# First block's modulation sums on VectorE, spread over its attention, and seven 2 MB buffers for expert weights

## The chip, the cores and the metric

The kernel runs on one core of one Trainium2 chip. The metric is the device time of one execution, in microseconds (us). Times of several executions are given by their median.

## The reference

Two transformer blocks over 256 tokens of width 1024. The first mixes with stick-breaking attention (SB, 8 heads) and the HGRN2 recurrence (HG, 4 heads), merges both through sigmoid gates, and then sends each token to 4 of 32 experts. The second block's norms are scaled and shifted by a modulation vector, `c_act @ w_ada + b_ada`, that depends on `c` alone:

```python
def hybrid_mixer(x, w_in, ...):
    sq, sk, sv, hq, hf, hi, hg, gate_sb, gate_hg = split(x @ w_in)
    o_sb = stick_breaking_attention(heads(sq), heads(sk), heads(sv))
    o_hg = hgrn2_recurrence(silu(hq), 1 - f, log(f), hi)      # f from hf
    o_hg = rms_norm(o_hg) * hgrn_norm_g * sigmoid(hg)
    merged = sigmoid(gate_sb) * (o_sb @ w_branch_sb) + sigmoid(gate_hg) * (o_hg @ w_branch_hgrn)
    return merged @ w_out

def first_block(x, ...):
    h = layer_norm(ALPHA * x + hybrid_mixer(x, ...))
    return layer_norm(ALPHA * h + moe(h, 32 experts, top 4))

def second_block(x, c, ...):
    mod = silu(c) @ w_ada + b_ada
    sh1, sc1, g1, sh2, sc2, g2 = split(mod, 6)
    h = rms_norm(x, norm1_g) * (1 + sc1) + sh1
    x = x + g1 * (mixed(h) @ w_out)
    h2 = rms_norm(x, norm2_g) * (1 + sc2) + sh2
    return x + g2 * ((silu(gt) * up) @ w_down)                # gt, up from h2 @ w_gu
```

All is float32. A product of TensorE is made of three (`mm3`): each operand is split into a high and a low part of a narrower type.

## The kernel before, in words

**Phase A** is the first block's mixer. `x @ w_in` is cut into units of 256 columns, 1 MB each. For one unit SP issues the load (`unit`, L207 to L218), ACT rounds the high half (`sh`, L164), DVE subtracts the low half (`sl`, L170, two pieces of 128x1024 for one unit), and PE runs 48 matmuls (`pj`, L174 to L176). `Weights.ahead` loads and splits units ahead of their use, over a ring of `NW` = 4 buffers of 1 MB, to which 4 buffers of the pool `w2` come later. Between the projections stand the pieces of the four HGRN heads (`hg_e`, `hg_s`, `hg_o`, `hg_n`: exponentials, scores, outputs, norm) and of the stick-breaking heads (`st_z`, `st_l`, `st_v`). Then come the gates GS (`gate_s`, 4 units), the branch `w_branch_sb` (2), the gates GH with `w_branch_hgrn`, and `w_out` (4), at whose end the router's logits are made and L704 makes the last small matmuls.

**Modulation.** The first part of the second block's modulation (columns 0 to 2048 of `w_ada`) is computed inside phase A: eight blocks of 128 rows, 1 MB each. `Modulation.step_sum` (L1264) loads block `k`, scales it by the block's 128 values of `c_act` (one for each partition) on ACT and adds it into `moda` on GpSimd; `finish_sum` later adds up over the partitions with PE. `mod_step` is called after `gate_s(1)`, `gate_s(2)`, `gate_s(3)`, after each SB branch and after each GH gate; what is left is done by `mod_step(8)` ahead of `experts`.

**Phase B** runs the 32 experts. Each has six units of 2 MB (four of `w_up`, two of `w_down`), 192 units and 403 MB in all. `big_unit` (L220) gives unit `t` one of `NW2` + `NW3` = 4 + 2 buffers, from the pools `w2` and `w3`. The pool `w3` is opened with phase B, where phase A's memory is free. The first four units can be loaded in phase A, into `w2`. Then SP has the rows `lng` and `lnb` of the layer norm (L261), `bdn`, small tables, and further units; SP and PE then read the register for the overflow branch (`flag`, L1106). Phase C is the second block.

**What sets the order.** In phases A and C a scheduler orders the instructions of each engine from their data. In phase B the order of PE and SP is that of the code (`manual_schedule`).

Of the kernel before, what the change touches and what calls it, by code (L numbers as in the profile page):

```python
# [10 lines left out]
F32 = mybir.dt.float32  # L11
# [3 lines left out]
OP = mybir.AluOpType  # L15
# [4 lines left out]
D = 1024  # L20
NW = 4
NW2 = 4
NW3 = 2
ALPHA = 2.0 ** 0.25
BIG = 1.0e30
NL = 7
# [114 lines left out]
def lines(ctx, tc, **kw):  # L141
    return Lines(ctx.enter_context(tc.tile_pool(**kw)))
# [75 lines left out]


def big_unit(E, src):  # L220

    t, n = E.wturn, NW2 + NW3
    E.wturn += 1
    at = NW2 - max(0, NW2 - (6 * NE - 1 - t) // n)
    pool, name = (E.w3, "u3") if at <= t % n < at + NW3 else (E.w2, "u2")
    u = pool.tile(list(src.shape), F32, name=name)
    E.nc.sync.dma_start(u, src)
    return u
# [62 lines left out]
def phase_a(E, A, open_h1, experts):  # L291
    nc, tc = E.nc, E.tc
    with ExitStack() as ctx:
# [145 lines left out]
        def copy_n(dst, i, ps):  # L439
            nc.scalar.activation(dst[:, :, i * 256:(i + 1) * 256], ps, AF.Copy)  # L440
# [100 lines left out]

        M = Modulation(E, A, ((0, 2048),), lambda n: tm.tile([P, 512], F32, name=n, tag="sg"))

        gate_f(0, pf0)
        gate_f(1, proj_n(HF + 256))
        silu_q(0, proj_t(HQ))
# [23 lines left out]
        hg_o(2)  # L570
        hg_s(3)
        nc.scalar.activation(sqT[:, 2:4], proj_t(SQ + 256), AF.Copy, scale=0.125)
        hg_n(2)
        hg_o(3)
        st_z(0)
        copy_n(sv, 0, proj_n(SV))
        hg_n(3)
        st_z(1)
        st_l(0)
        copy_n(sv, 1, proj_n(SV + 256))  # L580
        st_v(0)
        st_l(1)
        st_z(2)
# [6 lines left out]
            split_into(nc, ogh[:, c], ogl[:, c], ohT[:, c])  # L590

        gate_g(0, proj_t(HG))
        st_v(1)
        st_z(3)
        st_l(2)
        gate_g(1, proj_t(HG + 256))
        st_v(2)
        st_l(3)

# [8 lines left out]
        wsplit.load(wsplit.at + 4)  # L608
        ectx.close()
        h1 = open_h1()  # L610
        al2 = lines(ctx, tc, name="al2", bufs=1)

        def mod_step(n=1):
            for _ in range(n):
                M.step_sum(al2)

        gate_s(1)
        mod_step()
# [14 lines left out]
        for i in range(2):  # L633
            for jj, ps in enumerate(branch(sbw, osh, osl, i)):
                d = gs[:, i * 4 + 2 * jj:i * 4 + 2 * jj + 2]
                nc.vector.tensor_tensor(d, ps, d, op=OP.mult)  # L636
            mod_step()
        meh = al.tile([P, 8, T], F32R, name="meh", tag="xTh")
        mel = al.tile([P, 8, T], F32R, name="mel", tag="xTl")
        for i in range(2):  # L640
            ee = []
            for jj in range(2):
                e = tm.tile([P, 2, T], F32, name="sg")
                sigm(e, proj_t(GH + (2 * i + jj) * 256))
                ee.append(e)
                mod_step()
            if i == 0:
                x = al.tile([P, 2, D], F32, name="xr", tag="os")
                nc.sync.dma_start(x, xsrc)
                ln = LayerNorm(E, E.c)  # L650
            for jj, ps in enumerate(branch(hgw, ogh, ogl, i)):
                c = slice(i * 4 + 2 * jj, i * 4 + 2 * jj + 2)
                nc.vector.tensor_tensor(ee[jj], ps, ee[jj], op=OP.mult)
                nc.vector.tensor_add(gs[:, c], gs[:, c], ee[jj])
                split_into(nc, meh[:, c], mel[:, c], gs[:, c])
        mod_step(8)
        X = experts(tm)
        pl = pp.tile([P, T], F32, name="big")
        X.fold_ln(pp, "one")
# [184 lines left out]
def phase_b(E, A, X, acc):  # L844
    nc, tc = E.nc, E.tc
    up_u, dn_u, bup, it = X.up_u, X.dn_u, X.bup, X.it
    with ExitStack() as ctx:
# [13 lines left out]
        rp = lines(octx, tc, name="brt", bufs=1)  # L861
        lng = row_bcast(E, rp, A["ln1_g"], D, "lng")
        lnb = row_bcast(E, rp, A["ln1_b"], D, "lnb")
        bdn = b1.tile([NE, D], F32, name="bdn")
        nc.sync.dma_start(bdn, A["expert_b_down"][0])
        loaded = load_late(E, A, b1)
        gexp, selected, counted, rest = route(E, X, rp, pp, R)
# [212 lines left out]
def swiglu(nc, tm, ps, shape, out=None):  # L1080
    g = tm.tile(shape, F32, name="swg", bufs=1)
    s = tm.tile(shape, F32, name="sws", bufs=1)
    l = tm.tile(shape, F32, name="swl", bufs=1)
    act = (out or tm).tile(shape, F32, name="act")
    sl = (slice(None),) * (len(shape) - 1)
    nc.vector.tensor_scalar(g, ps[sl + (slice(0, None, 2),)], 7.0, None, op0=OP.min)  # L1086
    sg = nc.scalar.activation(s, g, AF.Sigmoid, scale=1.702)  # L1087
    nc.vector.tensor_scalar(l, ps[sl + (slice(1, None, 2),)], 7.0, -7.0, op0=OP.min, op1=OP.max)
    nc.vector.scalar_tensor_tensor(l, l, 1.0, g, op0=OP.add, op1=OP.mult)
    sw_last[:] = [sg, nc.vector.tensor_mul(act, l, s)]  # L1090
    return act


def overflow(E, A, X, b1, pp, R, acc, hT):
# [9 lines left out]
    with ExitStack() as ctx:  # L1104
        tm = lines(ctx, tc, name="otm", bufs=1)
        with tc.If(nc.values_load(R.flag[0:1, 0:1], min_val=0, max_val=1) > 0):  # L1106
            idr = tm.tile([P, P], F32R, name="idr")
            nc.scalar.activation(idr, E.ident, AF.Copy)
            for k in range(8):
                ps = pp.tile([P, 2, T], F32, name="g")  # L1110
                for a in range(2):
                    for n, part in enumerate((R.hh, R.hl)):
                        nc.tensor.matmul(ps[:, 0, a * P:(a + 1) * P], part[:, a, k * P:(k + 1) * P], idr,
                                         start=(a + n == 0), stop=(a + n == 2))
                nc.scalar.activation(hT[:, k], ps[:, 0], AF.Identity, bias=colv(E, "l1bp", k), scale=colv(E, "l1gp", k))
            with tc.For_i(0, NE, 1) as e:
                nc.vector.tensor_scalar(at, at, 1.0, None, op0=OP.add)
                for a in range(2):
                    w8 = tm.tile([P, NE], F32, name="w8", tag="idr")
                    nc.vector.tensor_scalar(w8, it, at, None, op0=OP.is_equal)  # L1120
                    nc.vector.tensor_mul(w8, w8, over[:, a])
                    wt = tm.tile([P, 1], F32, name="wt")
                    nc.vector.tensor_reduce(wt, w8, op=OP.add, axis=mybir.AxisListType.X)
                    aT = tm.tile([P, 8, P], F32, name="oaT")
                    for b in range(2):
                        for j in range(2):
                            br = tm.tile([1, 512], F32, name="br")
                            nc.sync.dma_start(br, bup[bass.ds(e, 1), (2 * b + j) * 512:(2 * b + j + 1) * 512])
                            nc.tensor.matmul(ups[:, j], ones[0:1], br, start=True, stop=False)
                        for k in range(8):  # L1130
                            u = tm.tile([P, D], F32, name="ou")
                            nc.sync.dma_start(u, wup[bass.ds(e, 1), k // 2 * 2 * P:(k // 2 + 1) * 2 * P, b * D:(b + 1) * D]
                                              .rearrange("o (p s) c -> s (o p) c", s=2)[k % 2])
                            for j in range(2):
                                nc.tensor.matmul(ups[:, j], hT[:, k, a * P:(a + 1) * P], u[:, j * 512:(j + 1) * 512],
                                                 start=False, stop=(k == 7))
                        act = swiglu(nc, b1, ups, [P, 2, 256], tm)
                        ps = pp.tile([P, 4, P], F32, name="t")
                        for j in range(4):
                            nc.tensor.transpose(ps[:, j], act[:, j // 2, (j % 2) * P:(j % 2 + 1) * P], E.ident)  # L1140
                        nc.scalar.activation(aT[:, 4 * b:4 * b + 4], ps, AF.Copy)
                    ys = [pp.tile([P, 512], F32, name="y", bufs=2) for _ in range(2)]
                    for c in range(8):
                        u = tm.tile([P, D], F32, name="ou")
                        nc.sync.dma_start(u, wdn[bass.ds(e, 1), c * P:(c + 1) * P, :].rearrange("o p c -> (o p) c"))
                        for j in range(2):
                            nc.tensor.matmul(ys[j], aT[:, c], u[:, j * 512:(j + 1) * 512], start=(c == 0), stop=(c == 7))
                    for j in range(2):
                        d = acc[:, a, j * 512:(j + 1) * 512]
                        nc.vector.scalar_tensor_tensor(d, ys[j], wt, d, op0=OP.mult, op1=OP.add)  # L1150
# [100 lines left out]
class Modulation:  # L1251
# [12 lines left out]
    def step_sum(self, pool):  # L1264

        nc, E = self.E.nc, self.E
        if not self.todo:
            return
        for k, u in self.load():
            if k == 0:  # L1270
                self.acc = pool.tile([P, self.n], F32, name="moda")
                nc.scalar.activation(self.acc, u, AF.Copy, scale=E.cact[:, 0:1])
            else:
                nc.scalar.activation(u, u, AF.Copy, scale=E.cact[:, k:k + 1])
                nc.gpsimd.tensor_tensor(self.acc, self.acc, u, op=OP.add)

    def finish_sum(self, pp, tag):
        nc, E, n = self.E.nc, self.E, self.n // 4
# [577 lines left out]
```

## Time and profile before

| | |
|---|---|
| three runs | 1573.3, 1574.02, 1581.15 us; median 1574.02 |
| profiled execution | 1583.92 us |
| its span | 1582.1 us |
| PE busy | 1472.4 us (93%), 8282 matmuls |
| DVE busy | 607.1 us (38%) |
| ACT busy | 418.4 us (26%) |
| GpSimd (POOL) busy | 72.9 us (5%) |
| read from memory | 516.46 MB |
| mean granted clock of PE | 0.962 |

The span is what the trace covers; the execution's own time is 1.8 us longer. Busy shares are means over phases that differ: phase A ends near 260 us and the experts' weights have landed by 1195 us. [...] L12 is line 12 of the kernel; `out<-in` are its names.

### The profile page before, as it was taken

The page shows a single profiled execution, that of the slowest core. Times are in us where ns is not written, and L with a number is a line of the kernel's source. Part 1 is how long each engine was busy: PE and PEld are TensorE (multiplying, and loading weights), DVE is VectorE, ACT ScalarE, POOL GpSimd, SP SyncE. Part 2 cuts the span into 40 slices and gives each one's busy share as a digit, 9 for nine tenths or more (in the row PEclk, how much of TensorE's full clock was granted, in tenths as well). Part 3 has the DMA queues.
Part 4 walks back from the last instruction along what each step waited for, and adds up shares of the span by engine and source line. Part 5 has one row for each costly group of instructions (what it writes and reads, how often), then busy time and mean ns, then how long its engine had stood idle before and what let it go on. Part 6 is the DMA issues. An engine that isn't in the chain of part 4 may idle for free.

```text
span 1582.1 us, 19654 instructions
## 1 busy us (share of the span) xinstructions
PE 1472.4 (93%) x8282; PEld 853.9 (54%) x8282; DVE 607.1 (38%) x1037; ACT 418.4 (26%) x675; POOL 72.9 (5%) x101
## 2 busy tenths in 40 slices
PE   8999699999989989999999999899897999999998
PEld 7999697333333333333333333233233876799998
DVE  6886877122111111211211211211215676665544
ACT  6558454001000000000001000000002565554442
POOL 0001512100000000000000000000000000000000
PEclk9999788999999999999999999999999998999999
DMA  8336766999999999999999999999998753275551
GB/s 294 125 102 236 265 207 260 374 422 430 430 429 429 430 429 430 430 429 429 430 430 429 430 429 430 430 430 429 430 430 304 248 194 107 94 253 187 187 187 54
DMA packets 106829, 518.84 MB, mean 328 GB/s; under 512 B 8144, under 2 KB 70352, under 8 KB 80112
## 3 DMA queue, kind: packets, MB, share of 16 engines
q1 hardware_dynamic: 106736, 517.53, 81.3%
q8 instruction: 67, 1.10, 0.3%
q14 instruction: 26, 0.21, 0.0%
HBM read 516.46 MB, written 1.05 MB: 327 GB/s over the span
## 4 chain that ended last, share of the span: by engine, by line
PE 59%; DMA 18%; DVE 2%; ACT 1%; issue 0%; DVEq 0%; ACTq 0%
PE up L989 20%; DMA u<-in_expert_w_down_dram 18%; PE y L1017 11%; PE y L1029 4%; PE gu L174 3%; PE gu L175 3%; PE gu L176 3%; PE g L951 2%; PE pd L174 1%; PE pd L175 1%; PE pd L176 1%; PE pj L174 1%; PE up L983 1%; PE pj L176 1%; PE pj L175 1%; PE o L1661 1%
## 5 line engine op out<-in xcount | busy, mean ns | idle before, releaser
L989 PE MATMUL up<-u,xg 128*64 128x512 f32 x2048 | 470.3, 601 | 1.7 <-DMA u<-in_expert_w_up_dram 1.7
L1017 PE MATMUL y<-u,aT 128*64 128x512 f32 x1024 | 267.1, 652 | 53.0 <-DMA u<-in_expert_w_down_dram 51.7
L989 PEld LDWEIGHTS up<-u,xg 128*64 128x64 f32 x2048 | 135.6, 137 | 265.5 <-issue 253.5
L170 DVE TENSOR_TENSOR sl<-u,sh 128x1024 fp32r<-128x1024 f32 (+3 forms) x160 | 208.4, 1308 | 120.2 <-ACT sh L164 118.9
L1017 PEld LDWEIGHTS y<-u,aT 128*64 128x64 f32 x1024 | 87.5, 149 | 231.2 <-issue 184.6
L164 ACT ACTIVATE sh<-u 128x1024 fp32r<-128x1024 f32 (+3 forms) x160 | 164.8, 1036 | 167.1 <-PE pj L175 39.6
L1086 DVE TENSOR_SCALAR swg<-up 128x512 f32<-128x512 f32 x32 | 22.1, 692 | 311.0 <-PE up L989 311.0
L1023 DVE COPY ys<-y 128x512 f32<-128x512 f32 x16 | 11.1, 692 | 276.6 <-PE y L1017 276.6
L174 PE MATMUL gu<-hTh,sh 128*128 128x256 f32 x352 | 99.5, 283 | 2.1 <-ACT modr L1307 2.1
L175 PE MATMUL gu<-hTl,sh 128*128 128x256 f32 x352 | 99.6, 283 | 0.0
L176 PE MATMUL gu<-hTh,sl 128*128 128x256 f32 x352 | 99.5, 283 | 0.0
L1087 ACT ACTIVATE sws<-swg 128x512 f32<-128x512 f32 x32 | 20.1, 629 | 262.9 <-DVE swg L1086 262.8
L1022 ACT ACTIVATE ys<-y 128x512 f32<-128x512 f32 x16 | 9.6, 597 | 280.7 <-PE y L1017 280.7
L1031 DVE TENSOR_TENSOR acc<-acc,y 128x512 f32<-128x512 f32 x62 | 42.7, 688 | 92.9 <-PE y L1029 92.9
L174 PE MATMUL pj<-xTh,sh 128*128 128x256 f32 x256 | 72.9, 285 | 4.6 <-DVE gs L636 4.6
L176 PE MATMUL pj<-xTh,sl 128*128 128x256 f32 x256 | 71.9, 281 | 0.0
L175 PE MATMUL pj<-xTl,sh 128*128 128x256 f32 x256 | 71.9, 281 | 0.0
L174 PEld LDWEIGHTS gu<-hTh,sh 128*128 128x128 f32 x352 | 68.2, 194 | 2.6 <-ACT modr L1307 2.6
L175 PEld LDWEIGHTS gu<-hTl,sh 128*128 128x128 f32 x352 | 66.8, 190 | 0.0
L176 PEld LDWEIGHTS gu<-hTh,sl 128*128 128x128 f32 x352 | 66.8, 190 | 0.0
L1029 PE MATMUL y<-ys,G 128*128 128x512 f32 x124 | 61.5, 618 | 0.0
L1007 ACT ACTIVATE aT<-t 128x512 f32<-128x512 f32 x32 | 19.1, 597 | 135.9 <-PE t L1005 135.9
(463 smaller groups left out, 2214.8 us busy)
## 6 DMA issues: line engine op xcount, KB each, us to landing
u<-in_expert_w_up_dram SPq DMA_DIRECT2D x128, 2048.0 KB, 18.8
u<-in_expert_w_down_dram SPq DMA_DIRECT2D x64, 2048.0 KB, 18.7
u<-in_w_in_dram SPq DMA_DIRECT2D x30, 1024.0 KB, 5.9
u<-in_w_ada_dram SPq DMA_DIRECT2D x24, 1024.0 KB, 6.3
u<-in_w_gu_dram SPq DMA_DIRECT2D x22, 1024.0 KB, 5.0
u<-in_w_down_dram SPq DMA_DIRECT2D x11, 1024.0 KB, 4.9
u<-in_w_out_dram SPq DMA_DIRECT2D x8, 1024.0 KB, 6.2
u<-in_w_branch_sb_dram SPq DMA_DIRECT2D x2, 1024.0 KB, 8.5
```

The costliest lines, as they stand in the source:

```text
L164: nc.scalar.activation(hi, src, AF.Copy)
L170: e.tensor_tensor(lo, src, hi, op=OP.subtract)
L174: nc.tensor.matmul(out, a[0], b[0], start=start, stop=False)
L175: nc.tensor.matmul(out, a[0], b[1], start=False, stop=False)
L176: nc.tensor.matmul(out, a[1], b[0], start=False, stop=stop)
L951: nc.tensor.matmul(ps[:, j], part[:, a, cs_], dm[:, a].rearrange("p e s -> p (e s)"), start=(n == 0), stop=(n == 7))
L989: nc.tensor.matmul(ps[i * 64:(i + 1) * 64, b].rearrange("q (m r) -> q m r", r=4), xgs[e // 4][:, k, sl], w.rearrange("p (m i r) -> p i m r ...
L1017: nc.tensor.matmul(y[oh][i * 64:(i + 1) * 64], aTs[e + i][:, 2 * b + r % 2, (r // 2) * 64:(r // 2 + 1) * 64], dn_u[e + i, b][:, r, oh * 51 ...
L1029: nc.tensor.matmul(pc, Gs[e // 2][:, a * P:(a + 1) * P], ys[:, oh], start=True, stop=True)
L1031: nc.vector.tensor_tensor(acc[:, a, c], acc[:, a, c], pc, op=OP.add)
L1086: nc.vector.tensor_scalar(g, ps[sl + (slice(0, None, 2),)], 7.0, None, op0=OP.min)
L1087: sg = nc.scalar.activation(s, g, AF.Sigmoid, scale=1.702)
```

## The change

`step_sum` does one instruction on VectorE for each block: the first scales block 0 into `moda`, the others multiply a block by its column of `c_act` and add `moda`. Five of the eight steps stand in the attention, three behind the gates GS. `NW3` becomes 3 and the units go round seven buffers in turn. To make room, `moda` lies in the pool `al`, `bdn` on a buffer of `ys`, swiglu's `swl` in `act`, and `br` (of the overflow branch) on `ou`.

```diff
-NW3 = 2
+NW3 = 3
 def big_unit(E, src):
-    t, n = E.wturn, NW2 + NW3
+    pool, name = (E.w2, "u2") if E.wturn % (NW2 + NW3) < NW2 else (E.w3, "u3")
     E.wturn += 1
-    at = NW2 - max(0, NW2 - (6 * NE - 1 - t) // n)
-    pool, name = (E.w3, "u3") if at <= t % n < at + NW3 else (E.w2, "u2")
...
         M = Modulation(E, A, ((0, 2048),), lambda n: tm.tile([P, 512], F32, name=n, tag="sg"))
+        def mod_step(n=1):
+            for _ in range(n):
+                M.step_sum(al)
...
         nc.scalar.activation(sqT[:, 2:4], proj_t(SQ + 256), AF.Copy, scale=0.125)
+        mod_step()
...
         copy_n(sv, 0, proj_n(SV))
+        mod_step()
...
         copy_n(sv, 1, proj_n(SV + 256))
+        mod_step()
...
         gate_g(0, proj_t(HG))
+        mod_step()
...
         gate_g(1, proj_t(HG + 256))
+        mod_step()
...
-        al2 = lines(ctx, tc, name="al2", bufs=1)
-        def mod_step(n=1):
-            for _ in range(n):
-                M.step_sum(al2)
         gate_s(1)
         mod_step()
...
                 nc.vector.tensor_tensor(d, ps, d, op=OP.mult)
-            mod_step()
...
                 ee.append(e)
-                mod_step()
...
-        mod_step(8)
         X = experts(tm)
...
-        bdn = b1.tile([NE, D], F32, name="bdn")
+        bdn = tm.tile([NE, D], F32, name="bdn", tag="ys", bufs=1)
...
-    l = tm.tile(shape, F32, name="swl", bufs=1)
-    act = (out or tm).tile(shape, F32, name="act")
+    l = act = (out or tm).tile(shape, F32, name="act")
...
-                            br = tm.tile([1, 512], F32, name="br")
+                            br = tm.tile([1, 512], F32, name="br", tag="ou")
...
             if k == 0:
                 self.acc = pool.tile([P, self.n], F32, name="moda")
-                nc.scalar.activation(self.acc, u, AF.Copy, scale=E.cact[:, 0:1])
+                nc.vector.tensor_scalar(self.acc, u, E.cact[:, 0:1], None, op0=OP.mult)
             else:
-                nc.scalar.activation(u, u, AF.Copy, scale=E.cact[:, k:k + 1])
-                nc.gpsimd.tensor_tensor(self.acc, self.acc, u, op=OP.add)
+                nc.vector.scalar_tensor_tensor(self.acc, u, E.cact[:, k:k + 1], self.acc, op0=OP.mult, op1=OP.add)
```

What this moves, as each engine's instructions stand in a row. SP at the attention before; `w_in` are the units of phase A, `w_ada` the modulation's blocks:

```order
L216 DMA u<-in_w_in_dram 128x8x256 x2
L216 DMA u<-in_consts_dram 128x1152
L216 DMA u<-in_w_in_dram 128x8x256 x14
L216 DMA u<-in_w_branch_sb_dram 128x4x512
L216 DMA u<-in_w_ada_dram 128x2048
L216 DMA u_1676<-in_w_ada_dram 128x2048
```

All fourteen `w_in` units stand ahead of the first `w_ada` block. The same place of SP now:

```order
L216 DMA u<-in_w_in_dram 128x8x256 x2
L216 DMA u<-in_consts_dram 128x1152
L216 DMA u<-in_w_in_dram 128x8x256 x7
L216 DMA u<-in_w_ada_dram 128x2048
L216 DMA u<-in_w_in_dram 128x8x256
L216 DMA u<-in_w_ada_dram 128x2048
L216 DMA u<-in_w_in_dram 128x8x256
L216 DMA u<-in_w_ada_dram 128x2048
L216 DMA u<-in_w_in_dram 128x8x256
L216 DMA u<-in_w_ada_dram 128x2048
L216 DMA u<-in_w_in_dram 128x8x256
L216 DMA u<-in_w_ada_dram 128x2048
```

The first five `w_ada` blocks now stand between `w_in` units; the other three follow ahead of the second unit of `w_branch_sb`, and none is left among the branches and the gates GH.

SP at the end of phase A before; `u` are units of 2 MB, `lng` waits for PE's L704:

```order
L227 DMA u_2621<-in_expert_w_up_dram 128x4096
L227 DMA u_2623<-in_expert_w_up_dram 128x4096
L1157 DMA kgrp<-in_consts_dram 128x128
L227 DMA u_2794<-in_expert_w_up_dram 128x4096
L261 DMA lng<-in_ln_g_dram 128x1024
L261 DMA lnb<-in_ln_b_dram 128x1024
L865 DMA bdn<-in_expert_b_down_dram 32x1024
L1160 DMA inv<-in_consts_dram 128x16
L1162 DMA ropeg<-in_ropeg_dram 128x64
L1164 DMA posi<-in_positions_dram 128x2x1
L227 DMA u_2796<-in_expert_w_up_dram 128x4096
L227 DMA u_2929<-in_expert_w_up_dram 128x4096
```

Five units stand ahead of `lng` (the first two of them above the rows shown), three behind it. The same place of SP now:

```order
L224 DMA u_2613<-in_expert_w_up_dram 128x4096
L733 DMA sraw<-in_consts_dram 128x64
L863 DMA bdn<-in_expert_b_down_dram 32x1024
L1157 DMA inv<-in_consts_dram 128x16
L1159 DMA ropeg<-in_ropeg_dram 128x64
L1161 DMA posi<-in_positions_dram 128x2x1
L258 DMA lng<-in_ln_g_dram 128x1024
L258 DMA lnb<-in_ln_b_dram 128x1024
L224 DMA u_2783<-in_expert_w_up_dram 128x4096
L224 DMA u_2785<-in_expert_w_up_dram 128x4096
L224 DMA u_2787<-in_expert_w_up_dram 128x4096
L224 DMA u_2919<-in_expert_w_up_dram 128x4096
```

Now four units stand ahead of `lng` (the first row is the fourth) and four behind it, and `bdn` with the small tables has moved ahead of it.

DVE inside the HGRN heads before (`ex`, `mk`, `sc` are a head's scores, `sl` the split of a weight, `sq`, `rs` a norm):

```order
L460 TENSOR_TENSOR ex<-ex,qT 128x128
L475 TENSOR_TENSOR mk<-mk 128x512
L476 TENSOR_TENSOR mk<-mk 128x256
L477 TENSOR_TENSOR sc<-mk 128x128
L474 TENSOR_TENSOR mk<-big,ksmask 128x1024
L170 TENSOR_TENSOR sl<-u,sh 128x1024
L475 TENSOR_TENSOR mk<-mk 128x512
L476 TENSOR_TENSOR mk<-mk 128x256
L147 TENSOR_SCALAR sq<-one 128x256
L477 TENSOR_TENSOR sc<-mk 128x128
```

Only the head's work and the weights' splits stand there. The same place of DVE now:

```order
L457 TENSOR_TENSOR ex<-ex,qT 128x128
L472 TENSOR_TENSOR mk<-mk 128x512
L1271 SCALAR_TENSOR_TENSOR moda<-u,cact,moda 128x2048
L473 TENSOR_TENSOR mk<-mk 128x256
L170 TENSOR_TENSOR sl<-u,sh 128x1024
L474 TENSOR_TENSOR sc<-mk 128x128
L147 TENSOR_SCALAR sq<-one 128x256
L471 TENSOR_TENSOR mk<-big,ksmask 128x1024
L150 TENSOR_TENSOR sq<-sq,rs 128x256
L472 TENSOR_TENSOR mk<-mk 128x512
```

The second step of `moda` stands inside a head's chain, ahead of a split and of `sc`.

## Rows read from the trace of the kernel before

**Rows 1.** Windows by stage: window, length, busy us of engines, granted clock, DMA share, GB/s.

```profile
57.00:100.00 43.00, 42.80 (x340) 40.85 (x339) 41.19 (x90) 19.57 (x34) 0.00 (x0) 1.00 0.27 88
100.00:158.00 58.00, 58.00 (x468) 53.25 (x467) 38.05 (x56) 44.63 (x57) 6.10 (x6) 1.00 0.56 197
158.00:260.00 102.00, 85.64 (x660) 81.94 (x659) 72.25 (x75) 47.93 (x61) 29.36 (x11) 0.87 0.67 247
260.00:289.00 29.00, 26.77 (x118) 13.57 (x120) 20.50 (x50) 9.27 (x13) 11.76 (x22) 0.82 0.70 261
289.00:1195.00 906.00, 845.82 (x3548) 296.50 (x3546) 159.21 (x261) 72.55 (x119) 18.59 (x51) 0.96 1.01 428
1195.00:1582.00 387.00, 364.07 (x2780) 320.52 (x2776) 236.90 (x434) 188.10 (x335) 3.34 (x5) 0.98 0.53 177
```

**Rows 2.** Waits of PE, 289 to 1195 us: total us, times, longest us.

```profile
PE y L1017 <- DMA u<-in_expert_w_down_dram: 51.7, 23, 3.9
```

**Rows 3.** Chain that ended last, in order of time: start us, us, what.

```profile
1174.56 19.92 DMA u<-in_expert_w_down_dram
```

**Rows 4.** Timeline of SP, 198 to 263 us: start us, us, queue, line, operation, count.

```profile
202.88 1.48 SPq L227 DMA_DIRECT2D u<-in_expert_w_up_dram  x1
...
245.65 0.39 SPq L227 DMA_DIRECT2D u<-in_expert_w_up_dram  x1
...
259.92 0.33 SPq L261 DMA_DIRECT2D lng<-in_ln_g_dram  x1
```

**Rows 5.** Line L1106 on SP's queue: ns min/median/max, first and last start us, forms.

```profile
L1106 SPq EVENT_SEMAPHORE  x10: 17/17/28, 279.0 to 288.6; - x10
```

**Rows 6.** Waits of PE, 150 to 262 us.

```profile
PE pj L176 <- DVE sl L170: 8.8, 1, 8.8
PE pj L174 <- DVE gs L636: 4.6, 1, 4.6
PE pj L174 <- ACT sg L366: 1.9, 1, 1.9
```

**Rows 7.** Line L1275 on POOL, columns of rows 5.

```profile
L1275 POOL TENSOR_TENSOR moda<-moda,u x7: 4568/4664/5298, 152.3 to 207.1; 128x2048 f32<-128x2048 f32 x7
```

**Rows 8.** Timeline of POOL: start us, us, engine, line, operation, count, idle before.

```profile
157.14 9.95 POOL L1275 TENSOR_TENSOR moda<-moda,u 128x2048 f32<-128x2048 f32 x2 [0.18 <-ACT u L1274]
...
178.17 4.92 POOL L1275 TENSOR_TENSOR moda<-moda,u 128x2048 f32<-128x2048 f32 x1 [0.57 <-ACT u L1274]
```

**Rows 9.** Timeline of DVE, same columns.

```profile
162.64 6.66 DVE L170 TENSOR_TENSOR sl<-u,sh 128x1024 fp32r<-128x1024 f32 x2
...
175.53 8.65 DVE L170 TENSOR_TENSOR sl<-u,sh 128x1024 fp32r<-128x1024 f32 x2
```

**Rows 10.** DVE groups by form, 57 to 150 us: busy us, mean ns, idle before.

```profile
L170 DVE TENSOR_TENSOR sl<-u,sh 128x1024 fp32r<-128x1024 f32 x20 | 24.4, 1222 | 7.5 <-ACT sh L164 7.4
...
L514 DVE SCALAR_TENSOR_TENSOR ss<-big,su 128x768 f32<-128x768 f32 x4 | 3.8, 956 | 3.4 <-ACT su L513 3.3
...
L170 DVE TENSOR_TENSOR ogl<-ohT,ogh 128x512 fp32r<-128x512 f32 x2 | 1.4, 688 | 0.7 <-ACT ogh L164 0.7
...
L367 DVE TENSOR_SCALAR gs<-gs 128x512 f32<-128x512 f32 x2 | 0.9, 427 | 2.5 <-ACT gs L366 2.5
```

**Rows 11.** Windows of 10 us in the gates' stage, columns of rows 1.

```profile
160.00:170.00 10.00, 1.77 (x8) 1.78 (x9) 10.00 (x5) 3.85 (x6) 7.01 (x2) 0.60 0.05 11
170.00:180.00 10.00, 10.00 (x81) 10.00 (x81) 6.55 (x5) 7.18 (x7) 6.43 (x2) 0.89 1.04 407
180.00:190.00 10.00, 5.39 (x30) 5.23 (x30) 7.64 (x5) 1.72 (x3) 3.09 (x1) 0.66 0.90 311
200.00:210.00 10.00, 10.00 (x91) 10.00 (x90) 9.47 (x10) 8.47 (x10) 2.86 (x1) 1.00 1.11 379
220.00:230.00 10.00, 10.00 (x64) 10.00 (x63) 6.89 (x12) 4.42 (x6) 0.00 (x0) 0.67 0.19 54
230.00:240.00 10.00, 10.00 (x73) 10.00 (x73) 4.85 (x7) 3.99 (x5) 0.00 (x0) 0.82 0.56 210
```

**Rows 12.** DVE groups by form, 150 to 220 us.

```profile
L170 DVE TENSOR_TENSOR sl<-u,sh 128x1024 fp32r<-128x1024 f32 x19 | 40.5, 2149 | 9.6 <-ACT sh L164 9.6
```

**Rows 13.** DMA issues on the page: line, engine, operation, count, KB each, us to landing.

```profile
u<-in_w_ada_dram SPq DMA_DIRECT2D x24, 1024.0 KB, 6.3
```

## Prediction

> **What bounds the kernel now.** I read the windows by stage first [rows 1]; the reader should see there two different limits. From 289 to 1195 us the DMA share is 1.01 at 428 GB/s: the expert weights stream and nothing else sets that stretch. PE waits in it for down weights 23 times, 51.7 us in all [rows 2], and the chain of waits ends it with the last down unit, issued at 1174.56 and 19.92 us on its way, so the stream ends at 1194.48 [rows 3]. The tail of 387 us behind it is the second block. Ahead of it lie 289 us whose limit is PE: 57 to 158 it is busy without a gap at a granted clock of 1.00. The stage of 158 to 260 differs: PE busy 85.64 of 102 us, clock 0.87, GpSimd 29.36. Phase A ends at 259.92, when SP, held until PE's last small matmuls are done, issues `lng` [rows 4]. What comes earlier there moves the whole stream and the tail with it, since the stream is a fixed 905.7 us (288.6 to 1194.48) [rows 3, 5] for 184 units of 2 MB.
>
> **Why 158 to 260 is slow.** PE's waits there [rows 6] are 8.8 us for DVE's `sl` split, 4.6 for DVE's `gs` product and 1.9 for ACT's `sg`: 15.3 us. The split is late because seven GpSimd adds of `moda` stand in that stage, each 4.6 to 5.3 us long [rows 7]. Put the timelines of the two engines side by side [rows 8, 9]: two adds run from 157.14 to 167.09, and in the same time two `sl` splits take 6.66 us; an add starts at 178.17, and two splits begun at 175.53 take 8.65. A split alone takes 1.22 [rows 10]. DVE does not wait on a semaphore there; its instruction runs stretched. The second loss is the clock [rows 11]: at 1.00 PE starts 91 matmuls in 10 us, so 0.11 us each; after the 8.8 us of waiting the window of 170 to 180 is granted 0.89 and holds 81; 180 to 190 at 0.66 has 5.39 us of work and 30 matmuls (49 would fit); 220 to 230, after the wait of 1.9, is at 0.67 with 64; 230 to 240 at 0.82 with 73; 160 to 170 has 8 in 1.77 us (16 would fit). That is 10 + 19 + 27 + 18 + 8 = 82 matmuls, 9.0 us. In all 24.3 us are lost.
>
> **Part 1: sums on VectorE.** The seven GpSimd adds and eight ACT scalings go; eight DVE instructions of 128x2048 come. No row shows one. Between 128x512 (688 ns) and 128x1024 (1222) a two-input DVE instruction costs 534 ns per 512 columns [rows 10], so 2048 columns give 1.222 + 2 x 0.534 = 2.29 us; the 128x768 scalar_tensor_tensor at 956 ns, scaled, gives 2.55. I take 2.3, nearer in kind of operands. The first, a tensor_scalar, is by 427 ns per 512 columns at most 1.7; I take 1.4. Sum 1.4 + 7 x 2.3 = 17.5 us, of which 6.9 (three steps) lie in the gates' stage.
> - Gates' stage. The 24.3 us come back if the stretching was their cause. DVE was busy 72.25 of 102 us there [rows 1], with splits at a mean of 2.15 us instead of 1.22 in it [rows 12], so it holds 6.9 us more. Price: 1.5 us, for one step that makes a split a little late. Bounds: 0; and 6.9 if all three steps are on the path. If the ACT wait of 1.9 us stays, its clock loss (45 matmuls, 5.0 us) stays too.
> - Attention. The order puts the five steps beside the HGRN heads, about 71 to 112 us on the clock of before. In 57 to 100 DVE is busy 41.19 of 43 us, spare 1.8; in 100 to 158 it has 19.95 of 58 spare, so about 4.1 in the first 12. Added 1.4 + 4 x 2.3 = 10.6 against 5.9 spare: a lag of 4.7 us at its worst, worked off later. PE is 42.80 of 43 busy beside a DVE that is 96% busy, so it runs some way behind DVE, and I take half the lag, 2.4, as PE waiting. One such wait costs clock as well: the 1.9 us wait was followed by 64 matmuls where 91 fit, 3.0 us. Together 5.4. Bounds: 0, if PE's distance covers the lag; 10.6 + 3.0 = 13.6, if every step reaches PE. [...]
> - The five w_ada loads now stand in SP's queue between the w_in loads, 1 MB each, so the queue's ring looks fewer w_in units ahead. DMA is 0.27 and 0.56 busy in the two stretches, and the load is late only if DVE holds a buffer; that price is inside the 5.4.
>
> GpSimd's queue loses its adds and holds no other work of that stage. ACT loses eight scalings of 128x2048; nothing waits longer for that.
>
> **Part 2: seven buffers.** The stream is full [rows 1], so a seventh buffer cannot shorten it; what it can do is start it earlier. Now e0 is issued at 202.88 and five units by 245.65 [rows 4]; then SP's flag load, and SP's semaphores run to 288.6 [rows 5], when the ninth unit, the stream's first, goes out: 28.7 us behind 259.92. In the new order four units stand ahead of `lng`, and e4 to e7 behind it, with no PE wait but e7's. Those four (8.4 MB) and `lng`, `lnb` (1.0 MB) at 428 GB/s are 22 us. A 1 MB load lands 6.3 us after its issue [rows 13], 2.4 of them its bytes at that rate, so 3.9 lie around the bytes, and about 26 us in all. Gain 2.7 (bounds 0, as SP may go on as late as now, and 6.5, without the 3.9). One new tail effect: the last unit in the third pool is released by PE near the end, so the second block's first loads start later; they have slack, price 0, bound +3.
>
> **Part 3: SBUF moves** (`bdn` on a `ys` buffer, `swl` merged with `act`, `br` on `ou`): no instruction more; the work of PE between the units covers them (DVE is busy 159 of 906 us there). Price 0; were it not covered there, the DMA-bound stream would still hide it.
>
> **Sum.** 24.3 - 1.5 - 5.4 + 2.7 = 20.1 us. The profiled execution took 1583.92 (span 1582.1), so a like one would take 1563.8; the runs' median is 1574.02, 9.9 lower, and I state the forecast on it: **1553.9 us**, -1.3%.
>
> **Rivals.**
> - All covered: the lags never reach PE. Gain 24.3 + 2.7 = 27, 1547. For it: DVE's spare after 100 us; against it: 96% before.
> - DVE becomes the bound of the attention: 13.6 in place of 5.4, and 3 more in the gates' stage. Gain 24.3 - 4.5 - 13.6 + 2.7 = 9, 1565. For it: 41.19 of 43. [...]
> - The change does not do what it says in its second half: the seventh buffer holds nothing early, since only four units are issued ahead of `lng`. Gain 17.4, 1556.6. For it: the order.
> - The other side: PE's clock in the attention. In 57 to 158 it has no gap and a clock of 1.00. If the waits behind the five steps come often enough that it stays at the level of 220 to 230 (64 in place of 91), 101 us become 144, +42.6, and the gain of 27 turns to a loss: 1574 + 15.6 = 1590. It decides from 64 of the 101 us on at that rate (64 x 0.42 = 27). Against it: five steps of 2.3 us lie about 10 us apart, and 200 to 210 shows a full clock some 10 us behind a wait.
>
> **How the numbers follow.** Forecast 0.45, all covered 0.2, DVE bound 0.17, buffer idle 0.11, clock 0.05, and 0.02 for unknown slips around 1574. A difference of 0.5%, 7.9 us, is about what a measurement of this kernel can tell from no change. Faster by more than that: the first, second, fourth cases whole and over half of the third, 0.86. Within it: the rest of the third and the slips, 0.09. Slower: 0.05. The range takes in the first two, the fourth and most of the third: 1546 to 1567.
>
> **What would show it.** In the changed profile: no GpSimd `moda` rows; eight DVE `moda` rows of about 2.3 us (first 1.4); all splits near 1.22; the 8.8 and 4.6 us waits gone and clock 0.95 or more from the gates to `lng`; `lng` issued near 242, SP's last drain some 26 us behind it, 905.7 from there to the last down unit, and a tail of 387. The forecast fails if DVE's splits stay stretched, if the attention's stretch grows by over 10 us, or if the stream takes another time for its 184 units.

## The result and the profile after

The changed kernel takes 1555.07 us (median of 4 runs, 1551.78 to 1556.98) against 1573.66 before: a ratio of 0.9872 with a 95% interval of 0.9838 to 0.9906. Run again in the study, beside other runs of the kernel before, it gave 1553.19 and a ratio of 0.9860 (0.9836 to 0.9884). The forecast of 1553.9 holds.

The windows by stage of the changed kernel, cut at its own ends of stages, answer to [rows 1] (window, length, busy time and count of PE, PEld, DVE, ACT and POOL, granted clock as a share of full speed, DMA share, GB/s):

```profile
57.00:100.00 43.00, 42.74 (x336) 40.59 (x336) 42.48 (x91) 18.79 (x31) 0.00 (x0) 1.00 0.45 148
100.00:158.00 58.00, 57.99 (x463) 52.84 (x463) 48.50 (x68) 39.37 (x58) 0.58 (x4) 1.00 0.66 235
158.00:239.00 81.00, 79.43 (x677) 76.53 (x675) 50.32 (x78) 40.63 (x58) 1.24 (x5) 1.00 0.66 233
239.00:265.00 26.00, 23.58 (x109) 12.17 (x110) 17.92 (x43) 8.38 (x12) 11.40 (x21) 0.87 0.90 364
265.00:1169.00 904.00, 844.69 (x3553) 294.49 (x3553) 161.13 (x264) 73.12 (x120) 18.61 (x52) 0.96 1.00 427
```

The stage behind 158 lasts 81 us where it lasted 102; PE is idle 1.6 us in it, not 16, and its clock is 1.00. DVE is 99% busy from 57 to 100, and PE does not mind: it is idle 0.3 us there. The waits of PE from 57 to 239 us (us, times, longest) show what is left in place of [rows 6]:

```profile
PE up L981 <- DVE lg L769: 0.8, 1, 0.8
PE pj L702 <- ACT lt L699: 0.5, 1, 0.5
PE big L672 <- ACT hTr L667: 0.3, 1, 0.3
PE one L483 <- DVE sc L474: 0.3, 1, 0.3
```

None is for a split. The tile `moda` (ns min/median/max, first and last start) shows the new instructions in place of [rows 7]:

```profile
L1271 DVE SCALAR_TENSOR_TENSOR moda<-u,cact,moda x7: 2343/2346/2348, 72.0 to 155.7; 128x2048 f32<-128x2048 f32 x7
L1269 DVE TENSOR_SCALAR moda<-u,cact x1: 1279/1279/1279, 60.4 to 60.4; 128x2048 f32<-128x2048 f32 x1
```

The groups of DVE by form, 150 to 240 us (busy us, mean ns, idle before), show the splits in place of [rows 12]:

```profile
L170 DVE TENSOR_TENSOR sl<-u,sh 128x1024 fp32r<-128x1024 f32 x25 | 30.3, 1221 | 12.2 <-ACT sh L164 12.2
```

A step costs 2.35 us and the first 1.28, and a split is back at 1.22 us from 2.15. At phase A's end the timeline of SP answers to [rows 4]:

```profile
238.36 0.33 SPq L258 DMA_DIRECT2D lng<-in_ln_g_dram  x1
```

The line of the flag on SP's queue answers to [rows 5]:

```profile
L1103 SPq EVENT_SEMAPHORE  x10: 17/17/28, 252.3 to 264.7; - x10
```

`lng` goes out at 238.36, 21.6 us earlier, and SP goes on 26.3 us behind it (before: 28.7).

### The profile page after: what moved, and what is told of

Same layout as the page of the kernel before. It is cut to its first block, busy times and chain, and to the rows that moved or that the text cites. A ratio compares the mean times of both kernels' runs of the same rounds, so it can differ in the third digit from the quotient of the medians.

```text
span 1551.9 us, 19635 instructions
## 1 busy us (share of the span) xinstructions
PE 1457.8 (94%) x8282; PEld 839.8 (54%) x8282; DVE 595.4 (38%) x1045; ACT 404.5 (26%) x667; POOL 38.8 (2%) x94
## 5 line engine op out<-in xcount | busy, mean ns | idle before, releaser
L1015 PE MATMUL y<-u,aT 128*64 128x512 f32 x1024 | 264.4, 647 | 51.5 <-DMA u<-in_expert_w_down_dram 51.1
L170 DVE TENSOR_TENSOR sl<-u,sh 128x1024 fp32r<-128x1024 f32 (+3 forms) x160 | 190.7, 1198 | 112.4 <-ACT sh L164 111.3
L1084 ACT ACTIVATE sws<-swg 128x512 f32<-128x512 f32 x32 | 20.1, 630 | 262.8 <-DVE swg L1083 262.7
```

Source lines behind the costliest of these rows:

```text
L170: e.tensor_tensor(lo, src, hi, op=OP.subtract)
L1015: nc.tensor.matmul(y[oh][i * 64:(i + 1) * 64], aTs[e + i][:, 2 * b + r % 2, (r // 2) * 64:(r // 2 + 1) * 64], dn_u[e + i, b][:, r, oh * 51 ...
```

## The experiments

First the ten runs together. "Attention" is the start of the last stick-breaking output matmul, "flag" SP's last semaphore there, "down" the start of the last matmul of the last down product, all in us of the profiled execution; the ratio is to the kernel before, with its interval. The two rows without a ratio stand for the two profiles told so far.

| kernel | attention | lng | flag | down | span | median | ratio |
|---|---|---|---|---|---|---|---|
| before, first profile | 141.0 | 259.9 | 288.6 | 1201.0 | 1582.1 | | |
| before again | 141.3 | 255.3 | 283.1 | 1195.4 | 1571.4 | 1575.9 | 0.9997 (0.9974, 1.0021) |
| changed, first profile | 142.8 | 238.4 | 264.7 | 1176.1 | 1551.9 | | |
| changed again | 142.2 | 237.7 | 264.4 | 1175.8 | 1546.9 | 1553.2 | 0.9860 (0.9836, 0.9884) |
| sums on DVE, old places, six | 141.1 | 240.1 | 268.8 | 1182.4 | 1558.6 | 1556.6 | 0.9871 (0.9834, 0.9907) |
| seven buffers alone | 141.6 | 260.5 | 285.4 | 1196.8 | 1579.5 | 1572.3 | 0.9961 (0.9934, 0.9988) |
| changed, six buffers | 142.3 | 233.2 | 265.5 | 1178.1 | 1555.1 | 1559.4 | 0.9897 (0.9861, 0.9932) |
| the same, old turn | 142.2 | 233.1 | 265.0 | 1178.9 | 1554.1 | 1557.6 | 0.9890 (0.9856, 0.9924) |
| sums on GpSimd, new places | 158.2 | 264.2 | 290.8 | 1202.2 | 1581.7 | 1581.8 | 1.0038 (1.0021, 1.0055) |
| changed, no sums | 140.8 | 236.3 | 262.8 | 1174.5 | 1547.1 | 1553.5 | 0.9867 (0.9840, 0.9894) |
| changed, units ahead | 141.7 | 239.1 | 263.7 | 1175.1 | 1557.5 | 1551.7 | 0.9841 (0.9817, 0.9865) |
| old places, units ahead | 139.9 | 237.4 | 261.9 | 1173.4 | 1551.3 | 1552.5 | 0.9855 (0.9819, 0.9891) |

Two things have to be known to read these columns. The executions differ ahead of the first step already: PE's 361st matmul, which stands before any step and is the same instruction in every run, starts at 54.8 and 55.1 us in the two profiles of the kernel before, at 55.8 and 55.3 in those of the changed kernel, and between 53.7 and 55.4 in the others. And `lng` tells of phase A's end in all rows but the two of the changed kernel with six buffers: there it goes out at 233, before PE's last small matmuls, the last of which starts at 237.45 and 237.35 us (changed kernel: 237.95 and 237.32).

**The kernel before, again.** No edit.

> The kernel before, unchanged, for a second profile. My theory: its profiled execution of 1583.92 us was a long one of this kernel; a new one takes about 1574, with the same waits of PE on DVE in the gates' stage (8.8 and 4.6 us, 13 to 15 together) and `lng` near 260, and a stream or a stage ahead of it that is some 5 to 10 us shorter. Rival: the stretch from the ninth unit to the last down unit is 905.7 us in every execution with six buffers, and seven buffers shortened it to 901.

The span is 1571.4, with the same waits (us, times, longest, 150 to 255 us):

```profile
PE pj L176 <- DVE sl L170: 8.9, 1, 8.9
PE pj L174 <- DVE gs L636: 4.8, 1, 4.8
PE pj L174 <- ACT sg L366: 1.2, 1, 1.2
```

What differs is the clock behind the third wait. Windows of 10 us, columns as above, to set against the last two of [rows 11]:

```profile
220.00:230.00 10.00, 10.00 (x89) 10.00 (x88) 6.93 (x13) 5.37 (x7) 0.00 (x0) 1.00 0.36 92
230.00:240.00 10.00, 10.00 (x89) 10.00 (x88) 9.34 (x12) 4.85 (x7) 0.53 (x1) 1.00 0.69 262
```

There 178 matmuls run where the first profile has 137, and `lng` is 4.6 us earlier, not near 260 as I expected. From flag to down it is 912.3 us (first profile: 912.4), so the stream does not vary between them; the tail behind down does, 376.0 against 381.1. The first profile was long by one fall of the clock and by its tail, not by the stream.

**The sums on VectorE alone, in their old places, with six buffers** (the edit to the kernel before):

```diff
-                nc.scalar.activation(self.acc, u, AF.Copy, scale=E.cact[:, 0:1])
+                nc.vector.tensor_scalar(self.acc, u, E.cact[:, 0:1], None, op0=OP.mult)
             else:
-                nc.scalar.activation(u, u, AF.Copy, scale=E.cact[:, k:k + 1])
-                nc.gpsimd.tensor_tensor(self.acc, self.acc, u, op=OP.add)
+                nc.vector.scalar_tensor_tensor(self.acc, u, E.cact[:, k:k + 1], self.acc, op0=OP.mult, op1=OP.add)
```

> The kernel before with the sums on VectorE in their old places and six buffers. My theory: what counts is that GpSimd no longer stretches DVE; the splits are back at 1.22 us, and eight steps, 17.7 us of DVE work in the gates' stage, fit in what the stretching gives back: 1554 to 1560 us. Rival: the spreading counts; in the old places the steps stand ahead of splits, PE waits there for DVE with a lower clock: 1562 to 1570.

0.9871: as far as a measurement tells, the whole gain of the change. All eight steps lie between 146.8 and 192.7 us, DVE is full from 150 to 170, and PE waits for no split or gate product. The splits are short again (DVE by form, 150 to 220 us, to set against [rows 12]):

```profile
L170 DVE TENSOR_TENSOR sl<-u,sh 128x1024 fp32r<-128x1024 f32 x22 | 26.6, 1220 | 9.6 <-ACT sh L164 9.6
```

The rival falls: the spreading is not needed. In the profile down starts 6.3 us later than in the changed kernel's first; 3.5 us of that lie between the attention's end and `lng`, where the granted clock fell to 0.83 in this execution (last section).

**The seven buffers alone** (`NW3 = 3`, the plain turn and the SBUF moves in the kernel before):

```diff
-NW3 = 2
+NW3 = 3
...
```

> The kernel before with the seven buffers and the SBUF moves alone; sums on ACT and GpSimd in their old places. My theory: 1569 to 1575 us, waits of 8.8 and 4.6 us and stretched splits as before. Rival: the seventh buffer brings a good part: 1563 to 1567.

0.9961, some 6 us by the median ratio with an interval of 2 to 10. The profile has the first profile's waits (8.8, 4.6, 1.9) and its splits are stretched as in [rows 12] (DVE by form, 150 to 220 us):

```profile
L170 DVE TENSOR_TENSOR sl<-u,sh 128x1024 fp32r<-128x1024 f32 x19 | 40.6, 2151 | 9.5 <-ACT sh L164 9.5
```

Against that first profile, whose `lng` is 0.5 us earlier, the flag is done 3.2 us earlier and down starts 4.2 earlier. So the buffers bring 3 to 4 us, and nothing of the gates' stage.

**The changed kernel with six buffers**, in the plain turn (`NW3 = 2`), and with the turn of the kernel before:

```diff
-NW3 = 3
+NW3 = 2
```

> The changed kernel with six buffers in place of seven. My theory: the sums bring nearly all; two units stand ahead of `lng` in place of none and two behind it in place of four, so 1554 to 1559 us. Rival: the seventh buffer brings a good part (the drain of 2.4 us and a stream 4.7 us shorter): 1562 to 1565.

1559.4, 0.4 us above what my theory gave and below the rival's range; 4 to 6 us behind the changed kernel by the ratios, whose intervals overlap. Part of it is a wait that the plain turn makes at the second block's start (waits of PE, 1160 to 1400 us):

```profile
PE modp L1291 <- DMA u<-in_w_ada_dram: 8.2, 4, 4.1
```

For the next run the turn alone was put back:

```diff
-    pool, name = (E.w2, "u2") if E.wturn % (NW2 + NW3) < NW2 else (E.w3, "u3")
+    t, n = E.wturn, NW2 + NW3
     E.wturn += 1
+    at = NW2 - max(0, NW2 - (6 * NE - 1 - t) // n)
+    pool, name = (E.w3, "u3") if at <= t % n < at + NW3 else (E.w2, "u2")
```

> The changed kernel with six buffers and the turn of the units of before, in which the last units avoid the third pool. My theory: of the 4 to 6 us by which six buffers in plain turn are behind seven, most are PE's 8.2 us of waiting for `w_ada` at the second block's start, which this turn avoids: 1554 to 1557 us, the wait for `w_ada` under 2 us. Rival (the seventh buffer itself brings them, in the stream): 1558 to 1561.

1557.55, between the two expectations: the wait for `w_ada` is gone, but the time fell by less than 2 us, within what the intervals leave open. What remains is in the table. From flag to down it is 912.3 to 913.9 us in the five profiles with six buffers and 911.4 to 911.7 in the seven with seven, and down starts at 1178.9 here and at 1178.1 in the plain turn, against 1175.8 and 1176.1. The seventh buffer is worth 2 to 3 us up to there.

**The sums on ACT and GpSimd in the new places** (the changed kernel with the instructions of before in `step_sum`):

```diff
-                nc.vector.tensor_scalar(self.acc, u, E.cact[:, 0:1], None, op0=OP.mult)
+                nc.scalar.activation(self.acc, u, AF.Copy, scale=E.cact[:, 0:1])
             else:
-                nc.vector.scalar_tensor_tensor(self.acc, u, E.cact[:, k:k + 1], self.acc, op0=OP.mult, op1=OP.add)
+                nc.scalar.activation(u, u, AF.Copy, scale=E.cact[:, k:k + 1])
+                nc.gpsimd.tensor_tensor(self.acc, self.acc, u, op=OP.add)
```

> The changed kernel with the sums back on ACT and GpSimd, in the new places, seven buffers. My theory: it is the adds' stretching of DVE that costs; four adds of 4.6 us now lie beside a DVE that is 96% busy, each takes some 3.5 us from it, and three still lie in the gates' stage: 1562 to 1575 us, attention's end 5 to 12 us later than before. Rival (the places alone bring the gain, whatever the engine): 1553 to 1560.

1581.79, slower than before, by more than I gave it. Waits of PE from 57 to 262 us:

```profile
PE pj L176 <- DVE sl L170: 7.2, 2, 4.2
PE big L520 <- DVE ss L513: 4.5, 1, 4.5
PE one L448 <- DVE sq L147: 3.7, 1, 3.7
PE one L484 <- DVE sc L474: 2.3, 1, 2.3
PE one L483 <- DVE sc L474: 1.8, 1, 1.8
```

The groups of DVE by form in the attention (57 to 160 us) show whose means the adds raise:

```profile
L472 DVE TENSOR_TENSOR mk<-mk 128x512 f32<-128x512 f32 x8 | 9.0, 1127 | 0.1
L473 DVE TENSOR_TENSOR mk<-mk 128x256 f32<-128x256 f32 x8 | 7.6, 956 | 0.2
L150 DVE TENSOR_TENSOR sq<-sq,rs 128x256 f32<-128x256 f32 x4 | 5.9, 1487 | 1.0 <-ACT rs L149 1.0
```

The same groups in the changed kernel (57 to 145 us), with no add beside them:

```profile
L472 DVE TENSOR_TENSOR mk<-mk 128x512 f32<-128x512 f32 x8 | 5.5, 684 | 0.0
...
L473 DVE TENSOR_TENSOR mk<-mk 128x256 f32<-128x256 f32 x8 | 3.4, 420 | 0.1
...
L150 DVE TENSOR_TENSOR sq<-sq,rs 128x256 f32<-128x256 f32 x4 | 1.7, 418 | 0.0
```

One add and what it does to DVE, from the two timelines (columns of [rows 8]):

```profile
71.81 4.56 POOL L1272 TENSOR_TENSOR moda<-moda,u 128x2048 f32<-128x2048 f32 x1 [44.49 <-ACT u L1271]
72.74 4.18 DVE L472 TENSOR_TENSOR mk<-mk 128x512 f32<-128x512 f32 x1
```

DVE's instruction of 0.69 us, begun beside the add, ends 0.55 us after it. So it is with every add: in this run and in the kernel before, seven adds stand against seven long DVE instructions (4.2 to 4.8 us here, 3.2 to 5.6 there), each begun while an add ran and ended after it. ACT's scalings, which came back with the adds, are not the cause: beside one of them alone, five splits of the kernel before kept their 1.22 us. The only DVE instruction there that began beside an add and kept its length is `gs<-pj,gs` (L636, 0.69 us at 174.92), which reads one operand from PSUM.

The attention ends 15 to 16 us later than in the changed kernel, which differs from this one only in the engines of the sums. With the sums on VectorE in their old places, this settles it: the gain is that of the engine. Why an add on GpSimd holds a VectorE instruction, no run here tells.

**No sums** (seven of the eight instructions cut to one column, which leaves nearly all of the modulation's first part out):

```diff
-                nc.vector.scalar_tensor_tensor(self.acc, u, E.cact[:, k:k + 1], self.acc, op0=OP.mult, op1=OP.add)
+                nc.vector.scalar_tensor_tensor(self.acc[:, 0:1], u[:, 0:1], E.cact[:, k:k + 1], self.acc[:, 0:1], op0=OP.mult, op1=OP.add)
```

> The changed kernel with seven of the eight sums reduced to one column, so the modulation's first part is left out; loads and order stay. My theory: the eight steps on VectorE cost 1.8 us in the attention and nothing behind it: 1 to 3 us below the changed kernel. Rival (the steps cost the 5.4 and 1.5 us that I had priced): 6 to 8 us below.

1553.51 against 1553.19 with them: my 1 to 3 us do not show in the medians. In the profile the attention ends at 140.8 in place of 142.2, but 0.9 us of this lie ahead of the first step. From the 361st matmul to the attention's end it is 86.4 us, against 87.0 and 86.9 with the sums, so the steps cost 0.5 to 0.6 us there; from there to `lng` it is 95.5 us, as with them. The rival is out.

**The three units ahead of `lng`:**

```diff
+        X.load_up(1, NW3)
         lng = row_bcast(E, rp, A["ln1_g"], D, "lng")
...
-        X.load_up(1, NW3)
```

> The changed kernel with the three units for the third pool issued ahead of `lng`, so that they fill the 15 us in which DMA stands still at phase A's end. My theory: three units of 4.9 us leave the stretch behind `lng`; the last of the eight still waits for PE's first two steps, so the ninth unit goes out 3 to 6 us earlier and the time falls by as much: 1549 to 1552 us. Rival (SP's wait for the flag and PE's first steps set that start): 0 to 1 us.

The median, 1551.68, lies in my theory's range; the profile bears out neither expectation. The timeline of SP shows the units moved up:

```profile
235.20 1.29 SPq L224 DMA_DIRECT2D u<-in_expert_w_up_dram  x3
239.14 0.33 SPq L258 DMA_DIRECT2D lng<-in_ln_g_dram  x1
...
252.55 17.46 SPq L224 DMA_DIRECT2D u<-in_expert_w_up_dram  x5
```

The eighth waits for PE's first steps until 252.55 in any case, and SP then for the flag until 263.7 (264.4 and 264.7 in the changed kernel's profiles), with DMA at 8% of its engines from 260 to 264. From `lng` to the flag it is 24.6 us (24.5 in the next run), against 26.3 and 26.7 in the changed kernel: the units bring some 2 us, between the 3 to 6 of my theory and the rival's 0 to 1. This execution had lost as much before, with 97.4 us from the attention's end to `lng` in place of 95.6 and 95.5 (last section). The ratio of 0.9841 (0.9817 to 0.9865) overlaps that of the changed kernel beside it.

**Old places and units ahead together**, seven buffers (the edit above, and the steps moved back; one of the five in the attention is shown):

```diff
         gate_g(0, proj_t(HG))
-        mod_step()
...
                 nc.vector.tensor_tensor(d, ps, d, op=OP.mult)
+            mod_step()
...
                 ee.append(e)
+                mod_step()
...
+        mod_step(8)
         X = experts(tm)
```

> The changed kernel (seven buffers, sums on VectorE) with the eight steps in their places of before, and the three units ahead of `lng`. My theory: the steps cost nothing in the gates' stage, where PE does not wait for them, and the 1.7 us of the attention come back; with the 1 to 2 us of the earlier units 1549 to 1552 us. Rival (spread steps are worth something, or the clock falls more often where DVE is full): 1554 to 1558.

The attention ends at 139.9 and down starts at 1173.4, the earliest of all, 2.4 us ahead of the changed kernel's second profile, of which 1.5 lie ahead of the first step; the time, 1552.46, is 0.5 us above the theory's range and below the rival's, and its ratio of 0.9855 is that of the changed kernel. No version here is shown to beat the change.

## Why the prediction was right

**What bounds the kernel** held. The stream takes nearly the same time with its start moved, 911.4 from flag to down (before: 912.4), and PE waits in it for the down weights as in [rows 2] (265 to 1169 us):

```profile
PE y L1015 <- DMA u<-in_expert_w_down_dram: 51.1, 23, 3.9
```

The prediction's 905.7 is a slip in the sum: from 288.6 to 1194.48 it is 905.9 us.

**The gates' stage** (24.3 less 1.5): right in kind, too large against a usual execution. From the attention's end to `lng` the changed kernel needs 95.6 us; the first profile of before needs 118.9, so 23.3 came back of the 22.8 that I forecast from it. But the second profile of before needs 114.0 and gives back 18.5. The difference is the fall of the clock at 220 to 240 us (0.67 and 0.82, against 1.00 in the second), which I had priced at 5.0 us from one execution and which the other does not have. I had put it down to the wait of 1.9 us ahead of it; the runs do not bear that out, since behind a wait of 1.2 us it stayed away and in three runs it came in part of the same matmuls with no wait (last section). The stage's own price of 1.5 us was not seen: the run without sums gains nothing there.

**The attention** (5.4): mis-sized. Its end moved by 1.8 us between the first profiles (141.0 to 142.8) and 0.9 between the second, but part of that lies ahead of the first step: from the 361st matmul on it takes 86.2 us in both profiles of the kernel before and 87.0 and 86.9 in the changed kernel's, 0.8 more. Taking the sums away gives back 0.5 to 0.6. DVE went to 42.48 of 43 us, but the lag hardly reached PE, whose longest wait there for DVE is 0.3 us, and no fall of its clock came: it is 1.00 in both stretches from 57 to 158. The step that failed is "I take half the lag" together with the added clock fall; the bound of 0 was nearer. The five steps also lay wider apart than the order told me, from 60.4 to 118.6 us and not from 71 to 112.

**The seven buffers** (2.7): right in size, 2.4 us from `lng` to the flag in the first profiles and 1.1 in the second, and some 1 us more from flag to down, which I had at 0. Alone, the buffers brought 3 to 4 us up to the last down product; the rival "the seventh buffer holds nothing early" is out.

**The sum.** Up to the last down product the second profile of before (1195.4) and the changed kernel's (1176.1, 1175.8) differ by 19.3 and 19.6 us (20.0 and 19.7 from the 361st matmul on); the forecast was 20.1. It fits so well by luck, because two errors cancel: 4.3 us too much for the gates' stage and 4.6 too much of a price for the attention. The tail was forecast at no change. It varies from 371 to 383 us over the twelve profiles, and nothing here ties that to the change.

**The rivals.** A lag that never reaches PE was closest to what the attention did. VectorE as the bound and the clock's fall in the attention did not come; what they look like is shown by the run with GpSimd in the new places, where PE waits for DVE and the granted clock is 0.96 from 57 to 100 and 0.94 from 100 to 158.

## What to carry to other kernels

Read the durations of an engine's instructions by form and by stage. Here the mean of a split differed between two stages (1.22 and 2.15 us) with no semaphore behind it, and the timeline of the other engines over the same microseconds said what held it: the adds, without which it was 1.22 again. An add on GpSimd that looked free, because GpSimd was idle otherwise, cost VectorE most of its own length (beside one of 4.56 us an instruction of 0.69 took 4.18); doing the same work on the busy VectorE in one instruction of 2.35 us was cheaper by far, in either place. When a loss is a clock fall, take a second profile before you put it into the sum: the two long waits came back to within 0.2 us here, the fall did not (178 matmuls from 220 to 240 us where there had been 137). And measure a stage from one instruction to another, not from the start of the span: the executions here differ by up to 2 us before the changed part begins.

## What the runs showed of the hardware beyond that

The granted clock fell to 0.83 with no wait ahead of it. In the run with the sums on VectorE in their old places PE never stands still from 190 to 220 us (windows of 10 us):

```profile
190.00:200.00 10.00, 10.00 (x87) 10.00 (x86) 7.79 (x8) 6.23 (x9) 0.00 (x0) 1.00 1.01 339
200.00:210.00 10.00, 10.00 (x76) 10.00 (x76) 8.21 (x14) 4.90 (x8) 0.00 (x0) 0.83 0.65 247
210.00:220.00 10.00, 10.00 (x73) 10.00 (x73) 5.04 (x7) 4.18 (x5) 0.00 (x0) 0.83 0.58 210
```

It is busy throughout, and still 25 matmuls short of the 87 a window; for a while they come 213 ns apart, where it was 118 just before (from 199.8 to 203.5 us). It is not the only one: in the same two windows the run with the units ahead has a granted clock of 0.92 and 0.91 (82 and 80 matmuls), and the one with old places and units ahead 0.83 in the first (77), both with PE busy 10.00 of 10 us. In all three it falls in the first matmuls of `w_out`, as it does in the first profile of before, which has its window of 230 to 240 [rows 11] from it. In the other five profiles with the sums on VectorE or left out it does not fall there. Why, no run tells.

And at a granted clock of 1.00 the same matmuls came at one of two rates, 4% apart (257 or 267 in 30 us), by execution and within one by stage. A window of 30 us in the second block's `gu` products, in the first profile of before:

```profile
1430.00:1460.00 30.00, 30.00 (x257) 30.00 (x256) 16.53 (x17) 14.19 (x16) 0.00 (x0) 1.00 0.58 182
```

And in its second profile:

```profile
1424.00:1454.00 30.00, 30.00 (x267) 30.00 (x267) 17.42 (x18) 14.64 (x17) 0.00 (x0) 1.00 0.63 208
```

The two profiles of the changed kernel differ likewise, 257 and 267, with tails of 375.8 and 371.1 us. In all twelve profiles the 1056 `gu` matmuls take 120.3 to 121.2 us (five of them) or 124.7 to 125.9 (seven). From 200 to 210 us it is the first profile of before that is the faster, 91 matmuls [rows 11] against 88 in its second. The two rates are part of the 12 us by which the tails scatter; its cause is open.
